# A hybrid decoder layer on one core: the first tile of x is loaded by ScalarE's queue, and one warming matmul stands behind the transpose of the norm's weights

## The chip, the cores and the metric

The kernel runs on one core of a Trainium2 chip. The metric is the time of one execution on the device, in microseconds (us); of several runs the median counts. The engines are TensorE (PE in the profile; PEld is its weight load), VectorE (DVE), ScalarE (ACT), GpSimd (POOL) and SyncE (SP). SyncE, ScalarE and GpSimd can each issue DMAs from a queue of their own; a row with a q behind the engine (SPq, ACTq) is such an issue.

## The reference

One decoder layer on 256 tokens of width 2048, all in float32:

```python
mix = hybrid_mixer(rmsnorm(h, norm_mix_pre), w_in, conv_w, conv_b, dt_bias, a_log, d_skip, ssm_norm_w, w_out)
h = h + rmsnorm(mix, norm_mix_post)
ff = squared_relu_mlp(rmsnorm(h, norm_mlp_pre), w_up, w_down)
h = h + rmsnorm(ff, norm_mlp_post)
```

`hybrid_mixer` multiplies the normed input by w_in (2048 x 12320), runs a causal convolution with a chunked state-space scan on one part of the columns and a dilated attention on the other, and multiplies both results by w_out. The change concerns only the beginning: `rmsnorm(h, norm_mix_pre)` and the first columns of the product with w_in.

## The kernel before

Every matrix product is made from numbers split in two: `hi`, rounded to the matmul's format by ScalarE (L144, L146), and `lo`, the rest, by VectorE (L145, L147). Products of hi and lo parts are summed in PSUM. The weights stream from HBM in tiles `raw` of 256 rows x 512 columns, issued by SyncE (L158, `fetch`), and are split as they come. TensorE multiplies nearly without a stop; which step it takes next is mostly set by a scheduler that knows priorities, and in some places by an order that is written by hand (`manual_schedule`).

The beginning (L607 to L612) is one of those places. It has no weights of the norm, no transposed x and no w_in yet, and makes them block by block, each block being KB = 2 slices of 128 columns of x and 256 rows of w_in:

- `ident` (L609, 64 KB, SyncE's queue) is the identity for TensorE's transposes; `pre` (L610, 8 KB, ScalarE's queue) holds the norm's 2048 weights as 16 rows of 128.
- `warm(n)` (L519) issues n matmuls of ones by ones, each of them two instructions, into a small PSUM tile that nobody reads. They keep TensorE busy while the first data is on its way. WARM = 6 stand at the very start; STAY = 4 stand behind the first transposes of x.
- `load_x(k0)` (L523) loads 256 columns of x for all 256 tokens (256 KB); `load(k0)` loads the block of w_in that goes with them, in two halves of 256 KB for the first three blocks. L570 to L573 issue block 0 and block 1 (x, w_in, x, w_in) and all of it goes through SyncE's queue, in this order, behind `ident`.
- L574 to L576 transpose `pre` on TensorE (L575) and copy it to `w_pre` on VectorE (L576).
- `turn_x(0)` (L549) transposes block 0 of x, four transposes of 128 x 128. `split_x` (L146, L147) scales the result by `w_pre` and splits it into the tile `ua`; `part` (L144, L145) splits w_in's half.
- In the loop behind, `products` (L468 for the hi part of w_in with both parts of x, L471 for the lo part) multiplies block k0, with `turn_x` of the next block between its two halves. So the transposes of block 1 come directly behind the first four L468 and four L471.

After the last block the first results are evicted from PSUM (L491 by ScalarE, L492 by VectorE, into `cT`), the next product with w_in begins, `squares` (L558) ends the sum of squares that the norm needs, and `raw_dt` (L647), the columns of w_in for the time steps, is loaded by ScalarE's queue and split into `wdt`. All this is ordered by the scheduler.

Of the kernel before, what the change touches and what calls it, by code (L numbers as in the profile page):

```python
# [44 lines left out]
BUFS = 5  # L45
RAWS = 4
LAG_DOWN = 3
WARM = 6
STAY = 4
SUMS = 10  # L50
FINE = 6
# [26 lines left out]
def hymba_layer(ctx: ExitStack, tc: tile.TileContext, x, norm_mix_pre, w_in, conv_w, conv_b, dt_bias, a_log,  # L78
                d_skip, ssm_norm_w, w_out, norm_mix_post, norm_mlp_pre, w_up, w_down, norm_mlp_post,
                consts, out):  # L80
    nc = tc.nc
    w_in, w_out, w_up, w_down = w_in[0], w_out[0], w_up[0], w_down[0]
    xt = x[0].rearrange("(t p) d -> p t d", p=P)
# [48 lines left out]
    def psmall():  # L132
        return psm.tile([P, NB], F32, name="ps")
# [7 lines left out]
    def split(hi, lo, src, scale=None):  # L141

        if scale is None:
            return (nc.scalar.activation(hi, src, AF.Copy),  # L144
                    nc.vector.tensor_tensor(lo, src, hi.bitcast(F32), op=ALU.subtract))  # L145
        return (nc.scalar.activation(hi, src, AF.Copy, scale=scale),  # L146
                nc.vector.scalar_tensor_tensor(lo, src, scale, hi.bitcast(F32), op0=ALU.mult, op1=ALU.subtract))  # L147

    def fetch(src, k0, c0, step=KB, into=None, pair=None):

        raw = wp.tile([P, KB, NB], F32, name="raw", bufs=RAWS) if into is None else into
        if pair is not None:
            nc.sync.dma_start(raw[:, 0], pair)
            loaded[:] = [nc.sync.dma_start(raw[:, 1], src[(k0 + 1) * P:(k0 + 2) * P, c0:c0 + NB])]
            return raw
        for j in range(0, KB, step):
            rs = slice((k0 + j) * P, (k0 + j + step) * P)
            loaded[:] = [nc.sync.dma_start(raw[:, j:j + step], src[rs, c0:c0 + NB].rearrange("(k p) n -> p k n", p=P))]  # L158
        return raw
# [58 lines left out]
    def parts():  # L218
        return [wp.tile([P, KB, NB], F32R, name=n, bufs=BUFS) for n in ("hi", "lo")]
# [242 lines left out]
    def features():  # L462
        return [bank().rearrange("p (b s) -> p b s", b=2) for _ in range(4)]

    def products(acc, hi, lo, k0, order):

        for f, j in order:
            nc.tensor.matmul(acc[f], hi[:, j, f * P:(f + 1) * P], u(k0 + j), start=k0 + j == 0, stop=False,  # L468
                             skip_group_check=True)
        for f, j in order:  # L470
            nc.tensor.matmul(acc[f][:, 0], lo[:, j, f * P:(f + 1) * P], u(k0 + j)[:, 0], start=False,  # L471
                             stop=k0 + j == NK - 1, skip_group_check=True)
# [38 lines left out]
    xs0 = xp.tile([P, NT, D], F32, name="xs0")  # L511
# [3 lines left out]
    def warm(n):  # L515

        p = psmall()
        for _ in range(n):
            nc.tensor.matmul(p[:, 0:P], ones, ones, start=True, stop=True)  # L519

    def load_x(k0):
        cs = slice(k0 * P, (k0 + KB) * P)
        nc.sync.dma_start(xs0[:, :, cs], xt[:, :, cs])  # L523

    def load_parameters():
        for r, src in enumerate((norm_mlp_pre, ssm_norm_w)):
            nc.sync.dma_start(rows[16 * r:16 * r + 16], src[0].rearrange("(k p) -> k p", p=P))
        nc.sync.dma_start(rows[32:64], conv_b[0].rearrange("(k p) -> k p", p=P))
        nc.sync.dma_start(crow, conv_w[0].rearrange("w (k p) -> (w k) p", p=P))
        nc.sync.dma_start(cst, consts[:, P:])  # L530
        for dst, src in ((bias_b, dt_bias), (a_b, a_log), (skip_b, d_skip)):
            nc.sync.dma_start(dst, src[0].partition_broadcast(P))
# [10 lines left out]
    def turn_x(k0):  # L543

        q = [psmall() for _ in range(KB)] if k0 % (2 * KB) else spare
        for f in range(KB):
            for t in range(NT):
                ks = slice((k0 + f) * P, (k0 + f + 1) * P)
                nc.tensor.transpose(q[f][:, t * P:(t + 1) * P], xs0[:, t, ks], ident)  # L549
        return q  # L550

    def split_x(k0, q, f):
        return split(u(k0 + f)[:, 0], u(k0 + f)[:, 1], q[f][:, :S], w_pre[:, k0 + f:k0 + f + 1])

    def squares(i):
        c, t = divmod(i, NT)
        junk = xp.tile([P, NB], BF16, name="junk", bufs=2)
        nc.scalar.activation(junk, xs0[:, t, c * NB:(c + 1) * NB], AF.Square, accum_out=sq1[:, t, c:c + 1])  # L558

    def first_block():  # L560
        acc = features()
        raws = {}

        def load(k0):
            raws[k0] = fetch(w_in, k0, COL_B, step=1 if k0 < FINE else KB)

        def part(k0, hi, lo, js):
            split(hi[:, js], lo[:, js], raws[k0][:, js])

        load_x(0)  # L570
        load(0)
        load_x(KB)
        load(KB)  # L573
        p = psmall()  # L574
        nc.tensor.transpose(p[:, 0:16], pre, ident[0:16, 0:16])  # L575
        nc.vector.tensor_copy(w_pre, p[:, 0:16])  # L576
        q = turn_x(0)
        warm(STAY)
        hi, lo = parts()
        for f in range(KB):  # L580
            split_x(0, q, f)
            part(0, hi, lo, slice(f, f + 1))
        for k0 in range(0, NK, KB):
            k1, k2 = k0 + KB, k0 + 2 * KB
            if k2 < NK:
                load_x(k2)
                load(k2)
            elif k2 == NK:
                load_parameters()
            products(acc, hi, lo, k0, [(f, 0) for f in range(4)])  # L590
            if k1 < NK:
                q = turn_x(k1)
            products(acc, hi, lo, k0, [(f, 1) for f in range(4)])
            if k1 == NK:
                break
            hi, lo = parts()
            if k1 >= FINE:
                part(k1, hi, lo, slice(0, KB))
            for f in range(KB):
                behind[:] = split_x(k1, q, f)  # L600
                if k1 < FINE:
                    part(k1, hi, lo, slice(f, f + 1))
            if k0 >= 4:
                squares(k0 // KB - 2)
        return acc

    nc.scalar.activation(rstd, half[:, 0:NT], AF.Copy)  # L607
    with tc.high_priority(offset=2 * AHEAD), tc.manual_schedule():
        nc.sync.dma_start(ident, consts[:, 0:P])  # L609
        nc.scalar.dma_start(pre, norm_mix_pre[0].rearrange("(k p) -> k p", p=P))  # L610
        warm(WARM)
        first = first_block()  # L612
# [837 lines left out]
```

## Time and profile before

| what | value |
|---|---|
| median of 3 runs | 1466.87 us (1465.23 to 1468.87) |
| the profiled execution's own time | 1465.38 us |
| its span, first to last instruction | 1463.5 us |
| mean granted clock of TensorE | 0.998 |
| DMA, mean over the span | 221 GB/s |

The profile is of one execution. In a timeline row the first number is the start in us from the begin of the span, the second the time from the first to the last of the merged instructions, then follow engine, line, operation, output and inputs, shapes and the count; a bracket gives the idle time before the row and what ended it. An L number is a line of the kernel. A row of the chain gives start, us, and what the end of the program hung on in this time. In a row of stretches the numbers behind each engine's busy time (x) are counts; the last three numbers are the granted clock, the share of the 16 DMA engines' time that was busy, and GB/s.

### The profile page before, as it was taken

The numbers are of one execution on the slowest core, as the hardware profiler recorded it, in microseconds if no ns is written. First come the engines' busy times: TensorE is split into PE (matmuls) and PEld (weight loads), VectorE is DVE, ScalarE is ACT, GpSimd is POOL, SyncE is SP. The second block draws the span as 40 slices with busy tenths as digits, with TensorE's granted clock in tenths as the row PEclk, the third lists the DMA queues.
The fourth block names the chain that finished last, engine by engine and source line by source line (L and its number), as shares of the span: only waits on it lengthen the run. The fifth ranks groups of instructions, "written<-read, shape, count | busy, mean of one in ns | idle before, by whom it ended". The sixth has DMA issues, their size and how long they took to land.

```text
span 1463.5 us, 20269 instructions
## 1 busy us (share of the span) xinstructions
PE 1452.7 (99%) x7129; PEld 1223.1 (84%) x7129; DVE 1255.5 (86%) x1864; ACT 888.0 (61%) x1214; POOL 143.3 (10%) x208
## 2 busy tenths in 40 slices
PE   9999999999999999999999999999999999999998
PEld 8888888888888888888887888888878888888886
DVE  6798797898887686689979999988888999999987
ACT  7475675465566556555557677655455766765653
POOL 0003100212010000000100011000111111101000
PEclk9999999999999999999999999999999999999999
DMA  8666666566886486688867798777788988778963
GB/s 272 209 203 181 179 186 190 176 181 177 234 234 205 133 243 200 194 263 252 252 192 242 207 309 238 218 216 225 224 235 285 266 244 247 208 240 250 311 205 115
DMA packets 168022, 323.53 MB, mean 221 GB/s; under 512 B 15168, under 2 KB 18096, under 8 KB 167920
## 3 DMA queue, kind: packets, MB, share of 16 engines
q1 hardware_dynamic: 144576, 272.50, 59.0%
q0 software_dynamic: 15616, 36.19, 12.3%
q10 hardware_dynamic: 7728, 13.54, 2.7%
q8 instruction: 56, 0.92, 0.2%
q14 instruction: 46, 0.38, 0.1%
HBM read 317.96 MB, written 40.41 MB: 245 GB/s over the span
## 4 chain that ended last, share of the span: by engine, by line
PE 94%; DVE 3%; DMA 2%; ACT 1%; issue 1%; SPq 0%; POOL 0%; DVEq 0%; ACTq 0%
PE acc L468 15%; PE acc L324 12%; PE acc L323 12%; PE acc L325 11%; PE acc L471 8%; PE acc L407 5%; PE acc L406 5%; PE acc L408 5%; PE ps L324 3%; PE ps L325 3%; PE ps L323 3%; PE ps L406 2%; PE ps L408 2%; PE ps L407 2%; DVE lo L145 1%; DMA raw<-pair 1%
## 5 line engine op out<-in xcount | busy, mean ns | idle before, releaser
L144 ACT ACTIVATE hi<-raw 128x1024 fp32r<-128x1024 f32 (+1 forms) x418 | 437.7, 1051 | 292.1 <-PE acc L325 94.2
L145 DVE TENSOR_TENSOR lo<-raw,hi 128x1024 fp32r<-128x1024 f32 (+1 forms) x418 | 508.7, 1220 | 99.6 <-ACT hi L144 94.4
L468 PE MATMUL acc<-ua,hi 128*128 128x512 f32 x600 | 163.5, 401 | 0.1
L468 PEld LDWEIGHTS acc<-ua,hi 128*128 128x128 f32 x600 | 105.7, 189 | 17.1 <-ACT hi L144 0.2
L144 ACT ACTIVATE hi<-e 128x1024 fp32r<-128x1024 f32 x61 | 64.8, 1063 | 80.9 <-DVE e L247 74.3
L323 PE MATMUL acc<-hi,ua 128*128 128x512 f32 x248 | 98.5, 397 | 0.0
L324 PE MATMUL acc<-lo,ua 128*128 128x512 f32 x248 | 96.8, 390 | 0.0
L471 PEld LDWEIGHTS acc<-ua,lo 128*128 128x128 f32 x600 | 88.2, 189 | 10.3
L325 PE MATMUL acc<-hi,ua 128*128 128x512 f32 x248 | 96.7, 390 | 0.0
L471 PE MATMUL acc<-ua,lo 128*128 128x256 f32 x600 | 90.8, 281 | 0.0
L323 PE MATMUL acc<-hi,sh 128*128 128x512 f32 x224 | 88.4, 395 | 0.0
L324 PE MATMUL acc<-lo,sh 128*128 128x512 f32 x224 | 87.3, 390 | 0.8 <-DVE lo L145 0.8
L325 PE MATMUL acc<-hi,sl 128*128 128x512 f32 x224 | 87.3, 390 | 0.0
L145 DVE TENSOR_TENSOR lo<-e,hi 128x1024 fp32r<-128x1024 f32 x61 | 74.3, 1217 | 0.0
L468 PE MATMUL acc<-uc,hi 128*128 128x512 f32 x240 | 68.4, 397 | 0.0
L406 PE MATMUL acc<-hi,ah 128*128 128x512 f32 x166 | 64.6, 389 | 0.0
L407 PE MATMUL acc<-lo,ah 128*128 128x512 f32 x166 | 64.6, 389 | 0.0
L408 PE MATMUL acc<-hi,al 128*128 128x512 f32 x166 | 64.6, 389 | 0.0
L145 DVE TENSOR_TENSOR lo<-uc,hi 128x1024 fp32r<-128x1024 f32 x38 | 46.2, 1221 | 15.2 <-ACT hi L144 15.0
L325 PE MATMUL acc<-hi,al 128*128 128x512 f32 x148 | 57.6, 389 | 0.0
L323 PE MATMUL acc<-hi,ah 128*128 128x512 f32 x148 | 57.6, 389 | 0.0
L324 PE MATMUL acc<-lo,ah 128*128 128x512 f32 x148 | 57.6, 389 | 0.0
(526 smaller groups left out, 3413.9 us busy)
## 6 DMA issues: line engine op xcount, KB each, us to landing
raw<-in_w_in_dram SPq DMA_DIRECT2D x181, 512.0 KB, 4.1
raw<-in_w_down_dram SPq DMA_DIRECT2D x79, 512.0 KB, 5.3
raw<-in_w_up_dram SPq DMA_DIRECT2D x65, 512.0 KB, 4.7
raw<-in_w_out_dram SPq DMA_DIRECT2D x39, 512.0 KB, 5.0
pair<-in_w_up_dram POOLq DMA_DIRECT2D x56, 256.0 KB, 5.3
raw<-pair SPq DMA_DIRECT2D x50, 256.0 KB, 4.3
pair<-in_w_down_dram POOLq DMA_DIRECT2D x46, 256.0 KB, 6.6
ha<-in_w_up_dram SPq DMA_DIRECT2D x20, 512.0 KB, 5.7
```

Of the source, the lines that this page charges most:

```text
L144: return (nc.scalar.activation(hi, src, AF.Copy), nc.vector.tensor_tensor(lo, src, hi.bitcast(F32), op=ALU.subtract))
L145: nc.vector.tensor_tensor(lo, src, hi.bitcast(F32), op=ALU.subtract))
L323: nc.tensor.matmul(dst, a_h[:, r, ts], hi[:, j], start=begin and j == 0, stop=False)
L324: nc.tensor.matmul(dst, a_h[:, r, ts], lo[:, j], start=False, stop=False)
L325: product[t] = nc.tensor.matmul(dst, a_l[:, r, ts], hi[:, j], start=False, stop=end and j == KB - 1)
L406: nc.tensor.matmul(dst, a_h, hi[:, j], start=own and first, stop=False)
L407: nc.tensor.matmul(dst, a_h, lo[:, j], start=False, stop=False)
L408: nc.tensor.matmul(dst, a_l, hi[:, j], start=False, stop=own and last)
L468: nc.tensor.matmul(acc[f], hi[:, j, f * P:(f + 1) * P], u(k0 + j), start=k0 + j == 0, stop=False, skip_group_check=True)
L471: nc.tensor.matmul(acc[f][:, 0], lo[:, j, f * P:(f + 1) * P], u(k0 + j)[:, 0], start=False, stop=k0 + j == NK - 1, skip_group_check=True)
```

## The change

```diff
-WARM = 6
+WARM = 5
...
-    def load_x(k0):
+    def load_x(k0, queue=nc.sync):
         cs = slice(k0 * P, (k0 + KB) * P)
-        nc.sync.dma_start(xs0[:, :, cs], xt[:, :, cs])
+        queue.dma_start(xs0[:, :, cs], xt[:, :, cs])
...
-        load_x(0)
         load(0)
         load_x(KB)
         load(KB)
         p = psmall()
         nc.tensor.transpose(p[:, 0:16], pre, ident[0:16, 0:16])
         nc.vector.tensor_copy(w_pre, p[:, 0:16])
+        warm(1)
         q = turn_x(0)
...
         nc.sync.dma_start(ident, consts[:, 0:P])
+        load_x(0, nc.scalar)
         nc.scalar.dma_start(pre, norm_mix_pre[0].rearrange("(k p) -> k p", p=P))
         warm(WARM)
```

The first tile of x leaves SyncE's queue and is issued by ScalarE, ahead of `pre`. The number of warming matmuls stays six; one of them now stands between the transpose of `pre` and the transposes of x. Lines behind the edits move by one (L647 is L648 after the change; L575 is L574).

At the start of the program TensorE's list reads as follows, before the change (L519 are the warming matmuls, the first L549 is block 0 of x, the second block 1):

```order
L519 MATMUL ps<-ones 128x128 x6
L575 MATMUL ps<-ident,pre 128x16
L549 MATMUL acc<-ident,xs_106 128x128 x4
L519 MATMUL ps<-ones 128x128 x4
L468 MATMUL acc<-ua,hi 128x512 x4
L471 MATMUL acc<-ua,lo 128x256 x4
L549 MATMUL ps<-ident,xs_106 128x128 x4
```

And after it:

```order
L519 MATMUL ps<-ones 128x128 x5
L574 MATMUL ps<-ident,pre 128x16
L519 MATMUL ps<-ones 128x128
L549 MATMUL acc<-ident,xs_106 128x128 x4
L519 MATMUL ps<-ones 128x128 x4
L468 MATMUL acc<-ua,hi 128x512 x4
L471 MATMUL acc<-ua,lo 128x256 x4
L549 MATMUL ps<-ident,xs_106 128x128 x4
```

Only the one L519 moved, from ahead of the transpose of `pre` to behind it. On ScalarE the list begins with L523, the load of x, and then has the load of `pre`, where it began with the load of `pre`; on SyncE the first L523 is gone and the rest keeps its order.

The scheduler, which plans from its own estimates, also answers with another order some 32 us into the program, where the first block's results are evicted. On ScalarE (L144 are splits of w_in, L558 squares, L491 evictions; - before, + after):

```order
 L146 ACTIVATE uc<-ps,par 128x256 x2
 L558 ACTIVATE junk,sq_94<-xs_106 128x512
-L144 ACTIVATE hi<-raw 128x1024
+L144 ACTIVATE hi<-raw 128x1024 x2
 L558 ACTIVATE junk,sq_94<-xs_106 128x512
 L144 ACTIVATE hi<-raw 128x1024
+L491 ACTIVATE cT<-acc 128x256 x4
+L144 ACTIVATE hi<-raw 128x1024
 L558 ACTIVATE junk,sq_94<-xs_106 128x512
-L491 ACTIVATE cT<-acc 128x256 x4
-L144 ACTIVATE hi<-raw 128x1024 x2
+L144 ACTIVATE hi<-raw 128x1024
```

One more split now stands ahead of the four evictions, and one of the squares behind them. VectorE's list moves in the same way: a split's `lo` and two small copies stand ahead of its four L492. On TensorE, in the next product with w_in (ua is x, hi and lo are w_in's parts):

```order
 L468 MATMUL acc<-ua,hi 128x512 x2
 L471 MATMUL acc<-ua,lo 128x256 x2
-L468 MATMUL acc<-ua,hi 128x512 x2
-L471 MATMUL acc<-ua,lo 128x256 x2
-L468 MATMUL acc<-ua,hi 128x512 x2
-L471 MATMUL acc<-ua,lo 128x256 x2
-L468 MATMUL acc<-ua,hi 128x512 x8
+L468 MATMUL acc<-ua,hi 128x512 x6
+L471 MATMUL acc<-ua,lo 128x256 x2
+L468 MATMUL acc<-ua,hi 128x512 x2
+L471 MATMUL acc<-ua,lo 128x256 x2
+L468 MATMUL acc<-ua,hi 128x512 x4
 L471 MATMUL acc<-ua,lo 128x256 x8
```

Four hi products of the following block, which write banks that are already free, moved ahead of the last products that wait for an evicted bank. From about 60 us on the lists of all engines are the same as before but for the tiles' numbers and, where `raw_dt` is loaded and split, one place.

## The prediction

> **What bounds the kernel now.** I began with the page's busy times and its chain.
>
> ```profile
> span 1463.5 us, 20269 instructions
> PE 1452.7 (99%) x7129; PEld 1223.1 (84%) x7129; DVE 1255.5 (86%) x1864; ACT 888.0 (61%) x1214; POOL 143.3 (10%) x208
> PE 94%; DVE 3%; DMA 2%; ACT 1%; issue 1%; SPq 0%; POOL 0%; DVEq 0%; ACTq 0%
> ```
>
> TensorE is busy for 1452.7 of 1463.5 us, and 94% of the chain that ended last is its matmuls. What is left is 10.8 us. The view of waits, for TensorE from 7.7 us to the end, tells how much of that lies behind the opening.
>
> ```profile
> PE ps L1318 <- ACT dg L1317: 2.0, 1, 2.0
> PE ps L1099 <- DVE ha L1090: 1.0, 1, 1.0
> PE ps L848 <- DVE mx L856: 0.9, 1, 0.9
> PE acc L324 <- DVE lo L145: 0.8, 1, 0.8
> PE acc L1373 <- ACT junk L1362: 0.4, 1, 0.4
> PE acc L1099 <- DVE ha L1090: 0.2, 1, 0.2
> ```
>
> Six waits, 5.3 us together, at lines that the change leaves alone. So the run is an opening of some 7.6 us, in which TensorE waits for the first data, and then a stream that hardly stops. A change of the opening moves the end by what it moves the start of that stream. The chain, asked for its first 8 us, shows what sets this start.
>
> ```profile
> 0.75 0.39 SPq L609
> ...
> 1.19 0.42 SPq L523
> ...
> 1.66 0.46 SPq L158
> ...
> 2.17 0.43 SPq L158
> ...
> 2.64 4.92 DMA xs<-in_x_dram
> 7.56 0.04 issue
> 7.61 0.44 PE ps L549 x2
> ```
>
> SyncE issues one DMA after another: the identity (L609), x's first tile (L523), two halves of w_in's first block (L158). Then comes x's second tile, issued at 2.64 and landed at 7.56, 4.92 us later, and its transposes at 7.61 open the stream. TensorE's timeline over the opening shows that its own work ends almost at the same moment.
>
> ```profile
> 1.06 2.93 PE L519 MATMUL ps<-ones 128*128 128x128 f32 x12 [1.06 <-DVE half L508]
> 3.92 0.23 PE L575 MATMUL ps<-ident,pre 16*128 16x16 f32 x1
> 4.26 0.66 PE L549 MATMUL acc<-ident,xs 128*128 128x128 f32 x4
> 4.75 1.06 PE L519 MATMUL ps<-ones 128*128 128x128 f32 x8
> 5.87 1.18 PE L468 MATMUL acc<-ua,hi 128*128 128x512 f32 x4
> 6.89 0.64 PE L471 MATMUL acc<-ua,lo 128*128 128x256 f32 x4
> ```
>
> A warming matmul is two instructions, so x12 is the six of before. The first products end at 6.89 + 0.64 = 7.53, and the second tile lands at 7.56: **two chains arrive within 0.03 us**. The stream starts earlier only if both get shorter; lengthening either moves it later.
>
> **The change, part by part.** The two chains start from these DMAs (issues in the first 2 us, with KB each and us from issue to landing) and ScalarE's rows.
>
> ```profile
> xs<-in_x_dram SPq DMA_DIRECT2D x1, 256.0 KB, 3.0
> raw<-in_w_in_dram SPq DMA_DIRECT2D x1, 256.0 KB, 3.5
> ident<-in_consts_dram SPq DMA_DIRECT2D x1, 64.0 KB, 2.1
> pre<-in_norm_mix_pre_dram ACTq DMA_DIRECT2D x1, 8.0 KB, 1.9
> ```
>
> ```profile
> 0.74 0.42 ACTq L610 DMA_DIRECT2D pre<-in_norm_mix_pre_dram  x1
> 4.74 0.47 ACT L146 ACTIVATE ua<-acc,par 128x256 fp32r<-128x256 f32 x1 [2.04 <-PE acc L549]
> 5.17 0.63 ACT L144 ACTIVATE hi<-raw 128x512 fp32r<-128x512 f32 x1
> ```
>
> *SyncE's queue loses one issue.* Everything behind the identity moves up one place: w_in's halves from 1.66 and 2.17 to 1.19 and 1.66, x's second tile from 2.64 to 2.17. That is 0.47 us. The same bytes must still arrive ahead of that tile, so its landing moves by between 0 and 0.47: to 7.09 at best, 7.56 at worst.
>
> *ScalarE's queue gains one issue.* x's first tile is issued at 0.74 instead of 1.19, and the norm's weights (`pre`) at 1.19 instead of 0.74. The table load behind them starts 0.45 later; it has 2 us of idle time before 4.74 as cover, and even with that gone it would cost no more than the 0.45.
>
> *When do the two land?* The first tile took 3.0 us, from 1.19 to 4.19, with 64 KB issued ahead of it; the second took 4.92 with 832 KB ahead. So landing grows with what is under way. From 0.74 the first tile lands at 3.74 if it takes 3.0 again, and at 5.66 if it takes 4.92. Now nothing is ahead of it on its queue, but w_in's first half is under way beside it from 1.19 on, so I take a little over 3.0: about 3.95. The weights, alone, took 1.9; issued at 1.19 they land at 3.09 at the earliest, and at 5.66 if they come in just behind a late tile. I take 4.0, close behind the tile, since the nearest row is the tile's own 3.0 and bytes issued ahead on a queue lengthened the landing above.
>
> What the transfers share is also in the stretches' rows (DMA share and GB/s last).
>
> ```profile
> 2.00:3.00 1.00, 1.00 (x7) 1.00 (x6) 0.00 (x0) 0.69 (x2) 0.00 (x0) 1.00 0.69 202
> 3.00:4.00 1.00, 1.00 (x6) 0.78 (x5) 0.00 (x0) 0.00 (x0) 0.00 (x0) 1.00 0.97 265
> 7.00:8.00 1.00, 0.92 (x9) 0.72 (x8) 0.42 (x1) 0.55 (x1) 0.00 (x0) 1.00 0.98 338
> ```
>
> The DMA engines are 69% busy from 2 to 3 us and 97% from 3 on: earlier issues can fill the first hole only.
>
> [...]
>
> *TensorE: five warming matmuls, the weights' transpose, then one.* The x12 row ends at 3.99 and two instructions are 0.46 of it (0.23 each, worked out under the clock), so five are over by about 3.5 us; then TensorE idles until the weights land. Their transpose starts at 4.0 + 0.07 (the gap that the x transposes show behind their tile, 4.19 to 4.26). The sixth matmul follows: two instructions at (1.06 - 0.28) / 7 = 0.11 us (x8 row, its last one 0.28), so 0.22, and about 0.11 behind the transpose. x's transposes start at 4.07 + 0.33 = 4.40 instead of 4.26: **+0.14**. Before, the six ran in time in which TensorE had nothing to do; the one moved now stands behind a landing. VectorE's copy of the weights still lies beside it, and ScalarE's first split still waits for the transposes, as at 4.74 before.
>
> The first chain then ends at 7.53 + 0.14 = 7.67 and the second between 7.09 and 7.56. The stream starts at 7.67 + 0.02 = 7.69 instead of 7.61, **+0.08 us**. *What is late next* is the weights, where it was the second tile.
>
> *The reordering near 32 us.* The program's order puts a split of w_in (hi and lo) ahead of the first block's evictions, and pairs of the next products ahead of the ones that need the freed banks.
>
> ```profile
> 32.07 1.19 ACT L491 ACTIVATE cT<-acc 128x256 f32<-128x256 f32 x4
> 32.73 1.41 DVE L492 TENSOR_TENSOR cT<-acc,cT 128x256 f32<-128x256 f32 x4
> 33.13 2.03 ACT L144 ACTIVATE hi<-raw 128x1024 fp32r<-128x1024 f32 x2
> 33.68 0.63 PE L468 MATMUL acc<-ua,hi 128*128 128x512 f32 x2
> 34.24 2.36 DVE L145 TENSOR_TENSOR lo<-raw,hi 128x1024 fp32r<-128x1024 f32 x2
> ...
> 43.20 0.69 DVE L145 TENSOR_TENSOR wdt<-raw_dt,wdt 128x512 fp32r<-128x512 f32 x1 [0.98 <-ACT wdt L144]
> ...
> 49.04 0.28 PE L654 MATMUL ps<-ua,wdt 128*64 128x256 f32 x1
> ```
>
> A lo split is 2.36 / 2 = 1.18, so VectorE's first eviction moves from 32.73 to about 33.9 and ends 1.41 / 4 = 0.35 later, near 34.3. The product that needs it stood at 33.68; four products are now ahead of it, (6.89 - 5.87) / 4 = 0.26 apart as in the opening, so it stands at 34.7. Cost: nothing, with 0.4 us to spare; if that cover is gone, at most the 1.2 us. raw_dt, the step weights, is issued behind one more split and split behind one more; what is made of it at 43.20 is needed at 49.04, and that is room for both. Behind this place the five engines' lists read alike but for tile numbers.
>
> **The sum.** +0.08 us. The profiled execution took 1465.38 us (span 1463.5 and 1.9 around it), which gives 1465.5. The median of the runs shown is 1466.87, 1.5 above that execution, so on its footing the forecast is 1466.95.
>
> **The rivals.**
>
> *Both chains get shorter.* If the weights land by 3.5 and the tile at 3.74, TensorE is through the sixth matmul at about 3.9, x's transposes start 0.36 earlier, the products end at 7.17, and with the second tile at 7.09 the stream starts at 7.17: -0.44 us, 1466.4. For it speaks the hole in the DMA share before 3 us; against it, that the weights now stand behind 256 KB. This is also all that the change could bring: the 0.47 of one issue.
>
> *Slower: the weights are late.* If sharing with w_in stretches the first tile to the second one's 4.92, the weights land at 5.66, x's transposes start at 5.66 + 0.07 + 0.33 = 6.06, +1.80, and the stream at 9.33: +1.72 us, 1468.6. It decides from a landing of the weights at about 3.95. For it speaks that before, the weights were never waited for (landed at 2.6, used at 3.92), and now they head the chain.
>
> *Slower: the clock.* The row of L519 gives the shortest, median and longest duration of the warming matmuls.
>
> ```profile
> L519 PE MATMUL ps<-ones x20: 275/421/582, 1.1 to 5.5; 128*128 128x128 f32 x20
> ```
>
> With a last one of 0.42 the x12 row goes at (2.93 - 0.42) / 11 = 0.23 an instruction, the x8 row at 0.11, so TensorE doubled its pace near 4 us, though the granted clock reads 1.00 in the stretches above. If the idle time from 3.5 to 4.07 put the doubling off past 7.6, the transposes (+0.4), the sixth matmul (+0.2), the four L468 (+1.0) and the four L471 (+0.5) would take 2.1 us more: 1469.0. Against it: TensorE is busy from 1.06 to about 3.5 in either order.
>
> [...]
>
> *The change does not do what it says:* the tile shares the same DMA engines from either queue, lands at 4.2 as before, and only the order differs. Then the weights land at 4.25 and the stream starts 0.33 later, 1467.2; I count it with the forecast.
>
> **How the numbers follow.** Forecast (the stream within 0.35 us of where it was) 0.63; both shorter 0.17; late weights 0.10; clock 0.05; something that I have not seen 0.05, 0.02 of it faster and 0.03 slower. All named cases lie within 2.2 us, and 0.3% is 4.4 us, about what a measurement of this kernel can tell from no change; so within 0.3% is 0.95, faster 0.02, slower 0.03. The runs shown spread from 1465.23 to 1468.87, more than any case moves the time, so the range is that spread with 0.44 off its low end and half a microsecond, for part of the late weights, on its high end: 1464.7 to 1469.4.
>
> **What would show it.** In the profile after: the weights' transpose should start near 4.1 and x's transposes near 4.4; TensorE should idle before the weights' transpose; the stream's first transposes should start between 7.2 and 8.0; the second tile's landing should be 0 to 0.47 earlier; no wait for an eviction (L492) near 34 us. The forecast would be wrong if the weights landed before 3.5 or after 4.5, if the warming pace did not double by 5 us, or if new waits of TensorE appeared past 30 us.

## The result and the profile after

| | before | after |
|---|---|---|
| median of 22 runs each | 1465.89 us (1461.95 to 1470.56) | 1469.67 us (1465.64 to 1474.84) |
| the profiled execution's own time | 1465.38 us | 1469.68 us |
| its span | 1463.5 us | 1467.9 us |

The ratio after to before is 1.0024, with a 95% interval of 1.0015 to 1.0033: the change costs 2.2 to 4.8 us. That is below the 0.3% that the prediction gave as the bound of "no change", but the interval leaves out zero, and the median lies 2.7 us above the forecast and 0.3 above the range.

Span and busy times, from the page of the kernel after:

```profile
span 1467.9 us, 20268 instructions
PE 1454.1 (99%) x7129; PEld 1225.0 (83%) x7129; DVE 1254.4 (85%) x1864; ACT 887.2 (60%) x1214; POOL 144.0 (10%) x208
```

TensorE has the same 7129 instructions; its busy time grew by 1.4 us and the span by 4.4. So it also waits some 3 us longer. The chain of the kernel after, asked for its first 8 us:

```profile
0.74 0.48 ACTq L523
1.23 0.03 issue
1.26 4.40 DMA pre<-in_norm_mix_pre_dram
5.66 0.14 issue
5.80 0.26 PE ps L574
6.05 0.72 PE ps L519 x2
```

Before, this chain hung on x's second tile. Now it hangs on the 8 KB of the norm's weights: issued at 1.26, landed at 5.66, and their transpose (L574, L575 before) at 5.80. TensorE's timeline after, up to the stream:

```profile
1.06 2.50 PE L519 MATMUL ps<-ones 128*128 128x128 f32 x10 [1.06 <-DVE half L508]
5.80 0.26 PE L574 MATMUL ps<-ident,pre 16*128 16x16 f32 x1 [2.23 <-DMA pre<-in_norm_mix_pre_dram]
5.98 0.80 PE L519 MATMUL ps<-ones 128*128 128x128 f32 x2
6.57 1.06 PE L549 MATMUL acc<-ident,xs 128*128 128x128 f32 x4
7.42 1.91 PE L519 MATMUL ps<-ones 128*128 128x128 f32 x8
8.99 2.05 PE L468 MATMUL acc<-ua,hi 128*128 128x512 f32 x4
10.84 0.74 PE L471 MATMUL acc<-ua,lo 128*128 128x256 f32 x4
11.42 0.60 PE L549 MATMUL ps<-ident,xs 128*128 128x128 f32 x4
```

Two things are to be seen. The bracket of the second row is the wait, 2.23 us. x's first tile is there from 4.80 on, but its transposes stand behind that of the weights in TensorE's list (no run tried the other order). And behind the wait the same instructions take nearly twice as long: the x8 row 1.91 us where it was 1.06, the four L468 2.05 where they were 1.18. TensorE runs at half pace until 11.05 us, where before it had doubled its pace at 3.91 (how these times are read stands under the table in the next section). So x's transposes start 2.31 us later (6.57 against 4.26), and from there to the stream it takes 4.85 us instead of 3.35. The stream starts at 11.42 instead of 7.61: **+3.81 us**.

Does that reach the end? One row of before and two of after, ahead of and behind the reordering near 32 us, answer that (L655 after is L654 before, which stands at 49.04 in the prediction).

```profile
31.92 0.27 PE L536 MATMUL ps<-ident,rows 64*128 64x64 f32 x1
```

```profile
35.55 0.27 PE L536 MATMUL ps<-ident,rows 64*128 64x64 f32 x1
...
52.69 0.28 PE L655 MATMUL ps<-ua,wdt 128*64 128x256 f32 x1
```

The lag is 35.55 - 31.92 = 3.63 us at the one and 52.69 - 49.04 = 3.65 at the other. Of the 3.81 us some 0.2 are made up by then, the rest stays, and the reordering between the two rows adds 0.02. The longest waits of TensorE from 12 us to the end, in the kernel after, and one shorter one:

```profile
PE ps L1319 <- ACT dg L1318: 2.0, 1, 2.0
PE ps L849 <- DVE mx L857: 1.3, 1, 1.3
PE ps L1100 <- DVE ha L1091: 0.9, 1, 0.9
PE ps L324 <- DVE lo L145: 0.8, 1, 0.8
...
PE acc L324 <- DVE lo L145: 0.3, 1, 0.3
```

The wait at L849 (L848 before) was 0.9 us and is 1.3, but over eleven profiles of this study it is between 0.7 and 2.8 without order, two of them of the unchanged kernel (0.9 and 2.8). It explains why single spans differ by a microsecond or two beside the opening, and nothing ties it to the change. Of the span's 4.4 us, 3.65 are thus the opening and 0.4 this wait. The rest is at L324 and at the very end. At L324 the waits for a split are 0.8 and 0.3 us where the kernel before had one of 0.8 (its second profile, below, has 0.8 and 0.5), and behind them the lag is 4.66 us (L1315 before at 1454.61, L1316 after at 1459.27). The last two matmuls then take 1.71 us before and 1.13 after, since before the clock went to half while they ran, at 1457.99; so the span ends 4.4 later.

### The profile page after: what moved, and what is told of

Its sections match the earlier page's. It is cut to its first block, busy times and chain, and to the rows that moved or that the text cites. A ratio compares the mean times of both kernels' runs of the same rounds, so it can differ in the third digit from the quotient of the medians.

```text
span 1467.9 us, 20268 instructions
## 1 busy us (share of the span) xinstructions
PE 1454.1 (99%) x7129; PEld 1225.0 (83%) x7129; DVE 1254.4 (85%) x1864; ACT 887.2 (60%) x1214; POOL 144.0 (10%) x208
## 4 chain that ended last, share of the span: by engine, by line
PE 86%; DVE 7%; DMA 3%; issue 1%; ACT 1%; POOL 0%; SPq 0%; ACTq 0%; DVEq 0%
PE acc L468 15%; PE acc L323 11%; PE acc L324 11%; PE acc L325 11%; PE acc L471 7%; PE acc L406 5%; PE acc L407 5%; PE acc L408 4%; DVE lo L145 4%; PE ps L324 3%; PE ps L325 3%; PE ps L323 3%; PE ps L406 2%; PE ps L407 2%; PE ps L408 2%; DMA raw<-pair 2%
## 5 line engine op out<-in xcount | busy, mean ns | idle before, releaser
L144 ACT ACTIVATE hi<-raw 128x1024 fp32r<-128x1024 f32 (+1 forms) x418 | 437.6, 1051 | 290.5 <-PE acc L468 92.4
L468 PE MATMUL acc<-ua,hi 128*128 128x512 f32 x600 | 164.4, 403 | 0.0
L468 PEld LDWEIGHTS acc<-ua,hi 128*128 128x128 f32 x600 | 106.3, 190 | 16.8
L144 ACT ACTIVATE hi<-e 128x1024 fp32r<-128x1024 f32 x61 | 64.9, 1063 | 79.9 <-DVE e L247 73.2
L471 PEld LDWEIGHTS acc<-ua,lo 128*128 128x128 f32 x600 | 88.4, 190 | 10.4
L324 PE MATMUL acc<-lo,ua 128*128 128x512 f32 x248 | 96.7, 390 | 0.0
L471 PE MATMUL acc<-ua,lo 128*128 128x256 f32 x600 | 90.9, 281 | 0.0
L324 PE MATMUL acc<-lo,sh 128*128 128x512 f32 x224 | 87.3, 390 | 0.3 <-DVE lo L145 0.3
L468 PE MATMUL acc<-uc,hi 128*128 128x512 f32 x240 | 68.4, 397 | 0.0
L324 PE MATMUL acc<-lo,ah 128*128 128x512 f32 x148 | 57.6, 389 | 0.0
```

What stands on the lines that cost most here:

```text
L144: return (nc.scalar.activation(hi, src, AF.Copy), nc.vector.tensor_tensor(lo, src, hi.bitcast(F32), op=ALU.subtract))
L324: nc.tensor.matmul(dst, a_h[:, r, ts], lo[:, j], start=False, stop=False)
```

## The experiments

The theory after the traces: the weights land late because, second on a queue beside a loaded one, they wait for more than the tile ahead of them; the pause of TensorE that follows also puts off the doubling of its pace; the two together are the loss. The rivals: the moved sixth matmul costs, or the reordering near 32 us does, or the clock was late by chance. These openings came out (landing of the weights; the longest pause of TensorE between 1.06 us and the stream; the x8 row of L519 and the first four L468; the time from which TensorE's clock is full; the start of the stream; all in us):

| kernel | weights landed | pause | x8 L519 | x4 L468 | full clock from | stream |
|---|---|---|---|---|---|---|
| before | 2.62 | 0.1 | 1.06 | 1.18 | 3.91 | 7.61 |
| before again | 2.68 | none | 1.19 | 1.16 | 5.36 | 7.52 |
| sixth matmul alone | 2.65 | none | 1.06 | 1.16 | 4.86 | 7.66 |
| all on SyncE's queue | 4.09 | 0.23 | 1.06 | 1.15 | 5.07 | 7.74 |
| the change, ten matmuls | 5.56 | none | 1.06 | 1.15 | 6.38 | 9.45 |
| weights first, then tile | 2.61 | 0.99 | 1.91 | 1.39 | 8.43 | 9.65 |
| before, two matmuls (three profiles) | 2.60 to 2.62 | 1.21 / 1.23 / 1.48 | 1.91 / 1.91 / 1.92 | 1.38 / 2.05 / 2.05 | 7.30 / 10.51 / 9.77 | 8.55 / 9.58 / 9.82 |
| identity on ScalarE's queue | 3.51 (identity 5.53) | 1.67 | 1.91 | 2.05 | 10.24 | 10.68 |
| queue alone (two profiles) | 5.63, 5.21 | 1.77, 1.36 | 1.91, 1.91 | 2.05, 2.05 | 11.66, 10.65 | 11.13, 10.70 |
| after | 5.66 | 2.23 | 1.91 | 2.05 | 11.05 | 11.42 |
| after again | 5.19 | 1.76 | 1.92 | 2.05 | 11.28 | 11.22 |

The last column but one comes from the list of clock changes that each trace keeps. No view prints this list, and the views count what lies ahead of its first entry as full clock; the first entry is what the column gives. It agrees with the pace of the rows: after, where it gives 11.05, four L468 take 2.05 us from 8.99 on and 1.18 from 11.77 on.

Where a time follows, it is the median of 11 or 12 runs against 29 or 35 of before on the same chip, unless it is called a single run.

**The queue alone.** The change without the moved matmul:

```diff
-WARM = 5
+WARM = 6
...
-        warm(1)
```

> Only the queue is changed: x's first tile on ScalarE's queue ahead of the norm's weights, all six warming matmuls in front as before. Theory A (the weights land behind the tile at about 5.7 us, TensorE idles from 4.0 to 5.7, and for that the clock opens late): weights' transpose at 5.7 to 5.9, warming matmuls behind x's transposes still 0.21 us apart, stream (transposes of x's second tile) 2.7 to 3.6 us later than before, ratio 1.002. Rival B (the sixth matmul behind the transposes is what costs): stream within 0.5 us of before, ratio 1.000.

1467.07 against 1465.19 us, ratio 1.0017 (1.0006 to 1.0027), so 0.9 to 4.0 us slower. Its opening:

```profile
5.76 0.25 PE L574 MATMUL ps<-ident,pre 16*128 16x16 f32 x1 [1.77 <-DMA pre<-in_norm_mix_pre_dram]
...
6.86 1.91 PE L519 MATMUL ps<-ones 128*128 128x128 f32 x8
```

Six matmuls ahead shorten the pause to 1.77 us and the weights still land at 5.63. The stream starts at 11.13: 3.52 of the 3.81 us are there with the queue alone. The rest, 0.29, is what the moved matmul can have added in this pair of profiles; in the second pair, below, the same difference is 0.52 (11.22 - 10.70). (The medians put this kernel's loss at 1.9 us and the change's at 3.8; the intervals overlap, and whether the two differ by more than this stays open.)

**The sixth matmul alone.** Before, with the matmul moved:

```diff
-WARM = 6
+WARM = 5
...
         nc.vector.tensor_copy(w_pre, p[:, 0:16])
+        warm(1)
```

> Only the warming matmul is moved behind the weights' transpose; x's first tile stays on SyncE's queue. Theory A: weights land at 2.6 us, their transpose at about 3.7, x's transposes at 4.2 to 4.4, clock open by 4 to 5 us, stream within 0.3 us of before, ratio 1.000. Rival B (the moved matmul costs): stream 1 us or more later, ratio above 1.0007.

1465.26 against 1465.19 us, ratio 1.0001 (0.9992 to 1.0009); the stream at 7.66. It costs nothing where the weights are early. That excludes the matmul as a cause of its own.

**The weights ahead of the tile** on ScalarE's queue, in the kernel after:

```diff
+        nc.scalar.dma_start(pre, norm_mix_pre[0].rearrange("(k p) -> k p", p=P))
         load_x(0, nc.scalar)
-        nc.scalar.dma_start(pre, norm_mix_pre[0].rearrange("(k p) -> k p", p=P))
```

> As the changed kernel, but the weights are issued first on ScalarE's queue and x's first tile behind them. Theory A: weights land at 2.6 to 2.9, the tile at 4.2 to 5.2 because it shares with w_in; TensorE is idle for 1 us at most; stream 0.2 to 1.0 us later than before if the clock opens in time (pace 0.11 by 5 us), 2 to 2.5 if it does not; ratio 1.0001 to 1.0015. Rival C (the tile's own late landing, shared with w_in, is the cost, not the weights behind it): the weights' place changes little, stream 3 us or more later, ratio 1.002.

1466.76 against 1465.19 us, ratio 1.001 (1.000 to 1.002). The DMA issues of its first 2 us, and TensorE's rows:

```profile
xs<-in_x_dram ACTq DMA_DIRECT2D x1, 256.0 KB, 4.3
...
pre<-in_norm_mix_pre_dram ACTq DMA_DIRECT2D x1, 8.0 KB, 1.9
```

```profile
5.49 1.11 PE L549 MATMUL acc<-ident,xs 128*128 128x128 f32 x4 [0.99 <-DMA xs<-in_x_dram]
6.39 1.91 PE L519 MATMUL ps<-ones 128*128 128x128 f32 x8
...
9.65 0.60 PE L549 MATMUL ps<-ident,xs 128*128 128x128 f32 x4
```

The weights take 1.9 us again, as before, and now the tile is late: second on this queue it takes 4.3 us, where it took 3.0 second on SyncE's queue. It landed at 5.44, past the 5.2 that theory A allowed. So it is not a trait of the 8 KB: here too, what stands second on ScalarE's queue beside SyncE's queue is late. A pause of only 0.99 us, after a full row of warming, went with half pace through the x8 row (1.91 us).

**Ten warming matmuls** ahead of the late weights, so that they land as late but TensorE never pauses:

```diff
-WARM = 5
+WARM = 10
```

> As the changed kernel with ten warming matmuls in front of the weights' transpose instead of five, so that TensorE is busy until about 5.4 us. Theory A: weights land at 5.7 as in the changed kernel, their transpose at about 5.8, but the clock has opened by then: sixth matmul and x's transposes at the pace of 0.11, stream 1.7 to 2.2 us later than before, ratio 1.0012 to 1.0015. Rival D (the late clock is chance, or has nothing to do with TensorE's idle time): pace still 0.21 behind 5.8 us, stream 3.6 us later, ratio 1.0025.

1466.80 against 1465.19 us, ratio 1.0012 (1.0004 to 1.0021), so 0.6 to 3.1 us slower.

```profile
1.06 4.64 PE L519 MATMUL ps<-ones 128*128 128x128 f32 x20 [1.06 <-DVE half L508]
5.70 0.26 PE L574 MATMUL ps<-ident,pre 16*128 16x16 f32 x1
...
6.87 1.06 PE L519 MATMUL ps<-ones 128*128 128x128 f32 x8
...
9.45 0.60 PE L549 MATMUL ps<-ident,xs 128*128 128x128 f32 x4
```

This run separates the two parts. The weights land at 5.56, nearly as in the kernel after, and the transpose starts 0.10 us earlier; but the x8 row is at full pace, and the stream starts at 9.45. So late weights alone cost 9.45 - 7.61 = 1.84 us, and the late clock 11.42 - 9.45 - 0.10 = 1.87 us.

**Two warming matmuls** in the kernel before: the pause without the late weights.

```diff
-WARM = 6
+WARM = 2
```

> The kernel of before with two warming matmuls at the start instead of six: every transfer as before (weights at 2.6 us, x's first tile at 4.2), only TensorE's idle time grows, from 0.3 us to about 2. It takes the clock by itself. Theory A (idle time in the opening makes the clock open later): pace still 0.21 us in the matmuls behind x's transposes, clock open at 7 to 9 us instead of 4 to 5, stream 1 to 2 us later, ratio 1.0007 to 1.0014. Rival D (the clock's opening does not depend on it): pace 0.11 by 5 us, stream within 0.2 us of before, ratio 1.000.

1466.52 against 1466.18 us, ratio 1.0003 (0.9992 to 1.0015): the time does not tell it from no change, although the stream started 2.21 us later in the profile. So it was profiled twice more.

> Two warming matmuls with the transfers of before, a second look at the clock. Theory A (idle time in the opening makes the clock open later): pace 0.21 us behind x's transposes, clock open between 6.5 and 10 us, stream 0.7 to 2.1 us later than in the profile of before. Rival D (the late clock of the first look was chance): pace 0.11 by 5 us, stream within 0.3 us of before.

> The same kernel, a third look; the same two expectations: theory A clock open between 6.5 and 10 us and stream 0.7 to 2.1 us late, rival D clock open by 5 us.

Single runs of 1464.15 and 1466.54 us, beside 1464.84 of before. In the first profile and in the second:

```profile
4.67 1.12 PE L549 MATMUL acc<-ident,xs 128*128 128x128 f32 x4 [1.48 <-DMA xs<-in_x_dram]
...
7.14 2.05 PE L468 MATMUL acc<-ua,hi 128*128 128x512 f32 x4
```

```profile
4.39 1.12 PE L549 MATMUL acc<-ident,xs 128*128 128x128 f32 x4 [1.21 <-DMA xs<-in_x_dram]
...
6.86 1.38 PE L468 MATMUL acc<-ua,hi 128*128 128x512 f32 x4
```

In all three the weights are early, TensorE pauses, and the x8 row is at half pace; how long it lasts differs by more than a microsecond for one and the same kernel (the stream at 8.55, 9.58 and 9.82). A pause therefore suffices for the late clock, without late weights. The clock's price is not one number, though, and the time of this kernel alone doesn't resolve it.

**Everything on SyncE's queue**, identity, tile, weights, w_in, in this order:

```diff
-        load_x(0)
         load(0)
...
         nc.sync.dma_start(ident, consts[:, 0:P])
-        nc.scalar.dma_start(pre, norm_mix_pre[0].rearrange("(k p) -> k p", p=P))
+        load_x(0)
+        nc.sync.dma_start(pre, norm_mix_pre[0].rearrange("(k p) -> k p", p=P))
```

> [...] Rival E (8 KB behind 256 KB on any queue land at about 5.6): weights' transpose at 5.7, stream 1.7 to 3.7 later, ratio 1.0012 to 1.0025.

1465.60 against 1466.18 us, ratio 0.9996 (0.9981 to 1.0010).

```profile
xs<-in_x_dram SPq DMA_DIRECT2D x1, 256.0 KB, 2.7
ident<-in_consts_dram SPq DMA_DIRECT2D x1, 64.0 KB, 1.9
pre<-in_norm_mix_pre_dram SPq DMA_DIRECT2D x1, 8.0 KB, 2.4
```

```profile
4.22 0.25 PE L574 MATMUL ps<-ident,pre 16*128 16x16 f32 x1 [0.23 <-DMA pre<-in_norm_mix_pre_dram]
...
5.20 1.06 PE L519 MATMUL ps<-ones 128*128 128x128 f32 x8
```

Here the weights stand behind the same 256 KB, but on one queue, and land at 4.09, 0.17 us behind the tile (3.92); rival E's 5.6 did not come. That is the "close behind the tile" of the prediction, and on this single queue it came true. The pause of 0.23 us did no harm to the clock (the x8 row at 1.06). The tile ahead is thus only a part of the delay; standing on a second queue made the rest in the kernel after (5.66). (No run left SyncE's queue empty beside it.)

**The identity on ScalarE's queue** behind the weights, the tile back on SyncE's, as a version that might have been faster:

```diff
-        nc.sync.dma_start(ident, consts[:, 0:P])
         nc.scalar.dma_start(pre, norm_mix_pre[0].rearrange("(k p) -> k p", p=P))
+        nc.scalar.dma_start(ident, consts[:, 0:P])
```

> The kernel of before with the identity (64 KB) moved to ScalarE's queue behind the weights, so that x's first tile is the first issue of SyncE's queue, at 0.75 us; nothing small stands behind a large transfer. Theory A: weights at 2.6 to 2.9, identity at 3 to 3.6, tile at 3.8 to 4.2, stream 0 to 0.45 us earlier than before, ratio 0.9997 to 1.000. [...]

1468.67 against 1466.18 us, ratio 1.0019 (1.0006 to 1.0031): slower, and the gain of theory A did not come. The DMA issues of its first 2 us:

```profile
raw<-in_w_in_dram SPq DMA_DIRECT2D x2, 256.0 KB, 4.3
xs<-in_x_dram SPq DMA_DIRECT2D x1, 256.0 KB, 3.2
ident<-in_consts_dram ACTq DMA_DIRECT2D x1, 64.0 KB, 4.3
pre<-in_norm_mix_pre_dram ACTq DMA_DIRECT2D x1, 8.0 KB, 2.8
```

The identity has only 8 KB ahead of it on its queue and takes 4.3 us (2.1 before, first on SyncE's). It landed at 5.53, 0.17 us behind w_in's first half (5.36), the second transfer of the other queue. About that distance holds for the weights in every kernel in which they are second on ScalarE's queue: 5.66 and 5.59 in the kernel after, 5.19 and 5.03 in it again, 5.63 and 5.46 and 5.21 and 5.02 with the queue alone, 5.56 and 5.39 with ten matmuls. In those five the distance behind their own tile is as even (0.80 to 0.89 us), so they alone don't tell which of the two transfers counts; the identity, which came 2.02 us behind the weights ahead of it, speaks for w_in's half. Even the first place on a queue was dearer with a large tile first on the other: the weights took 2.8 us here (1.9 before), and the identity 3.4 in the kernel after (2.1 before).

**The changed kernel, before, and the queue alone once more**, unchanged, to see how far one profile can be trusted:

> The changed kernel once more, for a second profile of its opening. Theory A: weights land at 5.4 to 5.8, their transpose follows within 0.2 us, clock open between 7 and 11.5, stream 2.5 to 4 us later than in the profile of before. Rival (the late weights of the first profile were chance): weights below 4.5, stream within 1 us of before.

> The kernel of before, a second look at its opening. Theory A (TensorE is busy from 1.06 us on but for 0.3 us): clock open between 3.9 and 5.5 us, weights landed at 2.6, stream within 0.3 us of the first profile. Rival D (the time of opening is chance in every kernel): clock open anywhere up to 11 us.

> x's first tile ahead of the weights on ScalarE's queue, all six warming matmuls in front, a second look. Theory A: weights land at 5.2 to 5.8 us, behind w_in's first half; clock open between 7 and 12 us; stream 1.5 to 3.7 us later than in the profile of before. Rival D: clock open by 5 us as in a kernel that does not idle, stream 1.5 to 1.9 us later.

Single runs of 1469.41, 1467.34 and 1467.44 us; the streams start at 11.22, 7.52 and 10.70. The weights land at 5.19 in the changed kernel this time, 0.2 us ahead of what was expected; the streams repeat to within 0.43 us, and the half pace through the four L468 stands in every profile of the changed kernel and of the queue alone. So the late opening belongs to the change and is no accident of one execution.

No version beat the kernel before.

## Why the prediction was wrong, point by point

- **What bounds the kernel: right.** The stream hardly stops, and the end moved by what its start moved: 3.81 us in the opening, 3.65 at 52 us, 3.78 between the medians. That the second tile and TensorE's own work end within 0.03 us of each other was luck of that execution, though: in the second profile of before the tile lands at 6.84 instead of 7.56, and TensorE's work alone sets the start.
- **The landing of the weights: wrong, and this is the step that failed.** "I take 4.0, close behind the tile" was 5.66. The tile itself was taken at 3.95 and landed at 4.80, 0.85 later; the weights then came 0.86 behind it instead of 0.05. The step counted what stood ahead on the weights' own queue and let the other queue only lengthen the tile a little. The runs show that the other queue counts too, and for more than a little: on a single queue the weights landed 0.17 us behind the tile, on the second queue 0.07 to 0.19 us behind w_in's first half. The upper bound, 5.66, agrees to the hundredth, but it was worked out from a tile of 4.92 us with the weights at once behind it; the tile took 4.1 and the weights came later, so the agreement is a coincidence. Of the signs of being wrong that the prediction named, two came: the weights landed after 4.5 us, and the pace had not doubled by 5.
- **The two slower rivals: each total near the measured one, and wrongly kept apart.** Late weights were priced at +1.72 us and measured at 1.84; a late clock was priced at +2.1 and measured at 1.87. Their sum is 3.8 and 3.7, and that is the result. The clock's total is partly luck: it left out the x8 row, which at half pace held the L468 back by 0.45 us, and took 0.5 for the L471 where 0.11 came (differences between the kernel after and the one with ten matmuls). Against the clock the prediction said that TensorE is busy from 1.06 to about 3.5 in either order. But in the kernel after the late weights made the pause (2.23 us), and the pace behind it was half (the x8 row at 1.91): the second followed from the first. As two separate cases they stood at 1468.6 and 1469.0; as one case a late landing would have stood at 1466.87 + 3.8 = 1470.7, on the forecast's own footing, and the range, which ended at 1469.4, would have had to reach there. An idle time of some 0.5 us, with which the clock's total reckoned, was not tried: the longest pause was at most 0.23 us or at least 0.99 in every profile.
- **The sixth matmul: right.** Alone it costs nothing (1.0001). Only behind late weights, at half pace, do the kernels with and without the move differ, by 0.29 and 0.52 us in the two pairs of profiles.
- **SyncE's queue: the later landings don't show the gain.** x's second tile landed at 6.86, 0.70 us earlier than 7.56 where 0 to 0.47 was allowed; but the kernel before again has it at 6.84 and the changed kernel again at 7.54, so a gain from the queue isn't shown. It opened nothing, since the other chain ended some 4.5 us behind it.
- **The reordering near 32 us: right.** The lag ahead of it and behind it differs by 0.02 us.
- **Both chains shorter:** no altered opening started its stream before 7.66, where the kernel before started at 7.61 and 7.52. The tile, on ScalarE's queue and issued 0.45 us earlier, took 4.1 us instead of 3.0 and landed some 0.6 later.
- **The footing:** the forecast stood 1.5 us above the profiled execution, after the median of three runs, 1466.87. Over 22 runs the median of before is 1465.89, 1.0 lower. That is why a miss of 3.7 us in the opening shows as one of 2.7 in the time.

## What to carry to other kernels

A small load that everything waits for should be first on its queue; put second on ScalarE's queue, it landed here with the second transfer of SyncE's queue, the 8 KB of the weights (5.66 beside 5.59 in the kernel after; 2.62 when they were first) as well as the 64 KB of the identity (5.53 beside 5.36). When a forecast makes an engine wait in the opening, ask in the same step what the wait does to that engine's pace: here the two belong to one case, and each is worth as much as the other (1.84 and 1.87 us). If a late load can't be avoided, work that keeps TensorE busy up to its landing can give back a part of the loss, here about half (ten warming matmuls: 9.45 instead of 11.42).

## What the runs showed of the hardware

- A pause between 0.99 and 2.23 us in the opening left the x8 row at half pace (1.91 or 1.92 us) in nine of nine profiles; with a pause of at most 0.23 us it was 1.06 to 1.19 in five of five. Nothing between these was tried.
- By the lists of the two traces the clock is full for 1454.08 us, from 3.91 on before and from 11.05 on after, and then at half.
- The price of a pause differed from one execution to the next. With two matmuls, pauses of 1.21, 1.23 and 1.48 us went with full clock from 7.30, 10.51 and 9.77 on. The first two differ by 0.02 us and their full clocks by 3.21, so the length of the pause alone does not give the price; what else sets it was not shown.
- The granted clock in the views reads 1.00 over the whole opening before (0 to 12 us) and after (0 to 11 us), also where the rows run at half pace (after, the x8 row at 1.91). Of the views, the pace of equal rows is the one to read at the start of a kernel.
- Later the granted clock does speak. In the kernel with the identity on ScalarE's queue TensorE waited 2.3 us at L848, near 456 us; here are the stretches behind that wait, and then those in the kernel before again, where the wait at this line was 2.8 us:

```profile
457.00:458.00 1.00, 1.00 (x6) 0.93 (x5) 0.54 (x5) 1.00 (x3) 0.00 (x0) 0.69 0.90 231
458.00:460.00 2.00, 2.00 (x6) 1.55 (x5) 1.40 (x7) 1.37 (x8) 0.00 (x0) 0.50 0.57 213
460.00:461.00 1.00, 1.00 (x4) 0.76 (x4) 1.00 (x5) 0.00 (x0) 0.00 (x0) 0.60 0.00 0
```

```profile
455.00:457.00 2.00, 2.00 (x11) 1.64 (x10) 1.99 (x9) 1.74 (x8) 0.00 (x0) 1.00 0.70 252
457.00:458.00 1.00, 1.00 (x10) 0.96 (x9) 1.00 (x6) 0.59 (x1) 0.00 (x0) 1.00 0.01 4
```

The clock (third number from the end) fell to 0.50 behind the shorter wait, for some 3.4 us (0.62 us in the row at 0.69, 2.00 at 0.50, 0.80 in the row at 0.60), and stayed at 1.00 behind the longer one. So the length of a wait alone does not tell whether the clock falls; what does was not shown. Such drops go with the spread of the runs: of the 35 runs of before on one chip, the 19 with a mean granted clock of 0.999 have a median of 1464.74 us, the 12 at 0.998 one of 1465.48, and the 4 below lie between 1467.25 and 1471.55. What else these runs differ in was not traced.
